# The last feed-forward block's gate and up projections as seven half-size products in place of eight

## The chip, the cores and the metric

The kernel runs on one core of a Trainium2 chip. The metric is the device time of one execution in microseconds; the median of three runs is compared. In the profile the engines are called PE (TensorE, matrix products), PEld (its weight loads), DVE (VectorE), ACT (ScalarE), POOL (GpSimd) and SP (SyncE, which issues the DMAs).

## What is computed

Two layers run over 512 latent and 256 context tokens of width 1024. Each layer has a feed-forward block, a token-mixing block and a second feed-forward block:

```python
def swiglu(h, wg, wu, wd):
    return (jax.nn.silu(h @ wg) * (h @ wu)) @ wd

def half_ffn(h, g, shift, scale, gate, wg, wu, wd):
    return h + 0.5 * gate * swiglu(modulate(rms_norm(h, g), shift, scale), wg, wu, wd)
...
        x = x + ml[5] * y_l
        x = half_ffn(x, g_norm[l, 2], ml[6], ml[7], ml[8], ffn_w_gate[l, 1], ffn_w_up[l, 1], ffn_w_down[l, 1])
        if need_ctx:
            ctx = ctx + mc[5] * y_c
            ctx = half_ffn(ctx, g_norm[l, 2], mc[6], mc[7], mc[8], ffn_w_gate[l, 1], ffn_w_up[l, 1], ffn_w_down[l, 1])
```

The hidden width is 2816, that is 22 tiles of 128. In the last layer `need_ctx` is false, so the fourth and last feed-forward block works on the 512 latent tokens alone; the other three work on all 768.

## The kernel before, in words

Activations lie transposed, as blocks of 128 channels by tokens. Every float32 operand of a projection is split into a high part (a rounded copy, made by ACT) and a low part (the rest, made by DVE), and each product is three matmuls: high weight by high data, high by low, low by high (`mm3`, L285). A weight tile arrives from memory as float32, 128 by 1024; `wsplit` (L200) casts it on ACT (`wh`) and subtracts on DVE (`wl`). So every weight tile costs both engines time, whatever the number of tokens.

`ffn` (L553) has two forms.

**Classical** (`classical`, L563). A hidden tile needs the projections of `h` by its gate weights and by its up weights: 2 projections of 8 channel blocks and 3 matmuls each, 48 matmuls, of 512 columns in the last block. Then silu of the gate on ACT, the product with up on DVE, and a split into high and low (`ah`, `al`). DVE and ACT split two weight tiles per hidden tile.

**Seven products** (L618 to L986; Winograd's variant of Strassen's form). The channels are halved (blocks 0 to 3 and 4 to 7), the tokens are halved, and gate and up are the two halves of the output. Of the eight block products seven are left, each of 4 channel blocks and 3 matmuls, 12 matmuls of half the tokens (`seventh`, L714): 84 matmuls of 384 columns for 768 tokens. For this, sums of halves of `h` are made and split once per block (`sums(j)`, L621, for four pairs of channel blocks; `sums_late`, L642, then overwrites a half of `h`), and sums of the weights for every hidden tile: `Weights` (L670) loads gate (`wr`, two buffers) and up (`wu`, one buffer) and makes four operands: `w1` the gate, `w2` two sums of up and gate (`ws`), `w3` what is left of up, `w4` half a tile of gate. These are four splits in place of two (three of 1024 columns and one of 512) and four DVE additions of 512 columns.

`Tile` (L725) holds a hidden tile. Its products p1, p6, p7 and p4 add into one PSUM bank B one after the other; between them ACT copies what has been added so far out of B (`take1` after p1, `take2` after p6, `take3` after p7), so the next one of them may begin only when that copy has ended. p2 goes to A; p5 and p3 go to C. `gate1`, `up2`, `act1`, `gate2` and `act2` put the pieces together on DVE, `high` and `low` split the result.

The order of PE, DVE and ACT in this form is written by hand: `chain` (L75) binds each instruction to the one before it on its engine. Hidden tiles go in groups of three (the last of four), `FAST`, L27. I call the tiles of a group a, b, c. PE's order in a group: p6, p2, p7, p5, p4 of a; p1, p2, p6, p5, p7 of b, p3 of a, p4 of b; the same for c, with p3 of b; p3 of c. While tile j runs, DVE and ACT make the weights of tile j+1 (`nx`), and finish tile j-1 (`p`). The gate weights of a tile are loaded when a buffer of `wr` is free, which is after the `w4` split two tiles before; its up weights are loaded when the split of the tile before's `w3` has ended.

After each group follows the **down** stage (L960): 8 output blocks, 3 matmuls per hidden tile each, with the update of the residual `xT` on DVE after each block. p1 of the next group's first tile is done in it.

In the kernel before, the last block does not take this form: `if not fast` (L602) runs the classical one in three groups of 8, 7 and 7 hidden tiles (`CHUNKS`, L25), each followed by its down stage through `residual` (L411). There the order on the engines is left to the scheduler.

The modulation vectors are worked off a queue beside the feed-forward blocks (`pump`, and `mod_step` in the seven-product form, two DVE steps `mr` and `mscr` each). In the trace the queue is empty when the last block's second hidden tile begins.

Of the kernel before, what the change touches and what calls it, by code (L numbers as in the profile page):

```python
# [24 lines left out]
CHUNKS = ((0, 8), (8, 7), (15, 7))  # L25
# [22 lines left out]
def tile_net(ctx: ExitStack, tc: tile.TileContext, a, out):  # L48
# [504 lines left out]
    def ffn(l, f, hin, streams, nxt, pre, npump, late={}):  # L553
# [5 lines left out]
        fast = w == T  # L559
        view = tv if fast else nv  # L560
        res = None

        def classical(m, ahead):  # L563
# [13 lines left out]
            else:  # L577
                pts = [ps(), ps()]
                for j in range(2):
                    project(full(pts[j]) if fast else plain(pts[j], cols), wgu[j], h)  # L580
                parts = [(banks(pts[0]), banks(pts[1]), pairs) if fast else
# [39 lines left out]
        def sums(j):  # L621

            X, Y = temp(), temp()
            lo, hi = slice(0, HALF), slice(HALF, T)
            c = slice(HALF * (j % 2), HALF * (j % 2) + HALF)
# [4 lines left out]
            ve.tensor_add(X, f32(h[j][0]), f32(h[j][1]))  # L630
            ve.tensor_add(Y, f32(h[j + 4][0]), f32(h[j + 4][1]))
# [7 lines left out]
            se.copy(U[j][0], Y)  # L639
            ve.tensor_sub(U[j][1], Y, f32(U[j][0]))  # L640

        def sums_late():  # L642

            hi = slice(HALF, T)
            for j in range(4):
                T1 = t1[j // 2][:, HALF * (j % 2):HALF * (j % 2) + HALF]
                se.copy(h[j][0][:, hi], T1)
                ve.tensor_sub(h[j][1][:, hi], T1, f32(h[j][0])[:, hi])

        chunks = FIRST if i == 0 else FAST  # L650
        sums_at = (2, 3, 4, 5) if i == 0 else (0, 1, 2)
        for ci in range(nslow):
# [14 lines left out]
            residual(down(m0, n), acts, gate, streams, None, view=tv)  # L667
# [41 lines left out]
        b11 = [tuple(t[:, 0:HALF] for t in h[k]) for k in range(4)]  # L709
        s1 = [tuple(t[:, HALF:T] for t in h[k]) for k in range(4)]  # L710
        b21 = [tuple(t[:, 0:HALF] for t in h[k + 4]) for k in range(4)]
        b22 = [tuple(t[:, HALF:T] for t in h[k + 4]) for k in range(4)]
# [1213 lines left out]
```

## Time and profile before

| | us |
|---|---|
| median of 3 runs | 2803.58 |
| range of these runs | 2801.41 to 2809.58 |
| the profiled execution's own time | 2802.09 |
| its span in the trace | 2800.0 |
| third feed-forward block, a group of three tiles with its down stage | 68.6 |
| last block, from its second hidden tile to PE's last matmul (2443.5 to 2795.3 in the trace) | 351.8 |

Times in the trace count from the start of the span. Nearly every instruction is recorded at line 66, a helper, so one goes by the names of tiles: `wl<-wr,wh` is the low part of a gate weight tile, `wl<-ws,wh` and `wl<-wu,wh` those of `w2` and `w3`, `w<-wr,w` that of `w4`; `s<-t` is `high` or `low` of a hidden tile; `t<-po` and `t<-ps` read PSUM. A timeline row gives start, duration, engine, operation and, in brackets, how long the engine stood idle before it and what ended that. DVE and ACT instructions overlap a little: the next one starts some 0.08 us before the one ahead of it ends.

### The profile page before, as it was taken

To read this page: it belongs to the slowest core of one execution; us is meant where nothing else is said; L and a number is where in the kernel's file an instruction comes from. 1 tells how busy PE (TensorE), PEld (TensorE's weight loads), DVE (VectorE), ACT (ScalarE), POOL (GpSimd) and SP (SyncE) were. 2 spreads that over 40 slices of the span, in tenths; PEclk is the share of its full clock that TensorE was granted. 3 is DMA by queue.
4 is the path that set the end of the run, shared out by engine and by line. 5 is a ranking of instruction groups with operands and counts; after the bars stand their busy time and mean duration, and the time that the engine had idled before them with its cause. 6 is when DMAs were issued, how large, how long until landed. Compare 5 with 4: busy or idle time off the path is not lost.

```text
span 2800.0 us, 38772 instructions
## 1 busy us (share of the span) xinstructions
PE 2705.3 (97%) x15364; PEld 2514.1 (90%) x15364; DVE 1949.8 (70%) x3279; ACT 1088.0 (39%) x1857; POOL 182.5 (7%) x224
## 2 busy tenths in 40 slices
PE   8999999999988999999999999999999999999999
PEld 5999999978878879999999899999988888888887
DVE  6756777777787877777778777776766788633333
ACT  5223333332477623333334333333332577322221
POOL 0000000010232200000000000000011132000000
PEclk9999999999999999999999999999999999999999
DMA  6322333215000332233333133333224102332232
GB/s 237 110 68 92 99 99 98 87 66 161 32 1 9 101 103 67 88 103 98 99 104 108 48 92 103 98 106 102 85 72 157 32 8 79 115 99 92 91 98 90
DMA packets 95268, 251.79 MB, mean 90 GB/s; under 512 B 11376, under 2 KB 40816, under 8 KB 95088
## 3 DMA queue, kind: packets, MB, share of 16 engines
q1 hardware_dynamic: 95088, 249.33, 28.1%
q8 instruction: 121, 1.98, 0.3%
q14 instruction: 59, 0.48, 0.1%
HBM read 247.19 MB, written 2.10 MB: 89 GB/s over the span
## 4 chain that ended last, share of the span: by engine, by line
PE 78%; DVE 10%; ACT 5%; DMA 3%; issue 2%; POOL 0%; SPq 0%; DVEq 0%; ACTq 0%; POOLq 0%
PE ps L66 46%; PE po L66 32%; DVE s L66 4%; ACT t L66 3%; DMA mr<-in_wm_dram 2%; DVE m L66 1%; ACT s L66 1%; DVE mr L66 1%; DVE t L66 1%; DMA wr<-in_wiN_dram 1%; DVE mscr L66 1%; DVE wl L66 1%; DVE xT L66 1%; ACT ph L66 1%; ACT ot L66 0%
## 5 line engine op out<-in xcount | busy, mean ns | idle before, releaser
L66 PE MATMUL ps<-s,wh 128*128 128x384 f32 (+2 forms) x4756 | 1153.0, 349 | 4.0 <-DVE t L66 2.1
L66 PEld LDWEIGHTS ps<-s,wh 128*128 128x128 f32 x4756 | 842.8, 189 | 73.1 <-DVE t L66 2.5
L66 PE MATMUL ps<-s,wl 128*128 128x384 f32 (+2 forms) x2378 | 714.3, 348 | 2.9 <-DVE wl L66 2.9
L66 PE MATMUL po<-s,wh 128*128 128x384 f32 (+2 forms) x2524 | 660.1, 343 | 2.4 <-ACT t L66 1.7
L66 PEld LDWEIGHTS po<-s,wh 128*128 128x128 f32 x2524 | 457.5, 188 | 18.3 <-ACT t L66 2.7
L66 PEld LDWEIGHTS ps<-s,wl 128*128 128x128 f32 x2378 | 433.6, 189 | 35.9 <-DVE wl L66 3.6
L66 PE MATMUL po<-s,wl 128*128 128x384 f32 (+2 forms) x1262 | 433.0, 343 | 7.2 <-DVE wl L66 7.2
L66 ACT CAST wh<-wr 128x1024 fp32r<-128x1024 f32 (+4 forms) x222 | 212.5, 959 | 413.8 <-PE ps L66 289.8
L66 DVE TENSOR_TENSOR wl<-wr,wh 128x1024 fp32r<-128x1024 f32 (+5 forms) x217 | 241.6, 1115 | 173.2 <-ACT wh L66 170.8
L66 DVE SCALAR_TENSOR_TENSOR xT<-ps,mod,xT 128x256 f32<-128x256 f32 (+1 forms) x392 | 213.1, 584 | 192.3 <-PE ps L66 191.9
L66 PEld LDWEIGHTS po<-s,wl 128*128 128x128 f32 x1262 | 237.8, 188 | 15.8 <-DVE wl L66 8.4
L66 DVE SCALAR_TENSOR_TENSOR mr<-mr,sb 128x1024 f32<-128x1024 f32 x128 | 156.1, 1219 | 6.7 <-DMA mr<-in_wm_dram 6.4
L66 PE MATMUL po<-s,s 128*128 128x256 f32 (+3 forms) x880 | 141.9, 314 | 11.5 <-ACT s L66 5.0
L66 ACT ACTIVATE t<-t 128x384 f32<-128x384 f32 x106 | 55.7, 525 | 243.4 <-DVE t L66 243.4
L66 ACT COPY t<-po 128x384 f32<-128x384 f32 (+1 forms) x161 | 76.9, 478 | 185.4 <-PE po L66 184.3
L66 PEld LDWEIGHTS po<-s,s 128*128 128x128 f32 x880 | 128.1, 192 | 19.4 <-ACT s L66 7.2
L66 DVE TENSOR_TENSOR t<-ps,t 128x384 f32<-128x384 f32 (+3 forms) x91 | 55.3, 607 | 119.3 <-PE ps L66 119.3
L337 POOL TENSOR_TENSOR s<-s,t 128x256 f32<-128x256 f32 x19 | 17.5, 921 | 1750.2 <-ACT t L66 1749.8
L66 ACT CAST s<-t 128x768 fp32r<-128x768 f32 (+2 forms) x129 | 88.0, 684 | 100.2 <-DVE t L66 100.0
L66 DVE TENSOR_TENSOR s<-t,s 128x768 fp32r<-128x768 f32 (+2 forms) x129 | 98.7, 767 | 37.9 <-ACT s L66 37.5
L66 DVE SCALAR_TENSOR_TENSOR mscr<-mr,sb 128x1024 f32<-128x1024 f32 x96 | 117.3, 1222 | 7.9 <-DMA mr<-in_wm_dram 6.3
L66 PE MATMUL po<-s,w 128*128 128x384 f32 x636 | 119.4, 336 | 0.0
(186 smaller groups left out, 3275.2 us busy)
## 6 DMA issues: line engine op xcount, KB each, us to landing
mr<-in_wm_dram SPq DMA_DIRECT2D x128, 512.0 KB, 3.7
wr<-in_wg_dram SPq DMA_DIRECT2D x88, 512.0 KB, 3.5
wu<-in_wu_dram SPq DMA_DIRECT2D x53, 512.0 KB, 3.5
t<-in_wd_dram SPq DMA_DIRECT2D x56, 384.0 KB, 3.5
wr<-in_wu_dram SPq DMA_DIRECT2D x35, 512.0 KB, 3.5
wr<-in_wiT_dram SPq DMA_DIRECT2D x22, 512.0 KB, 3.9
wr<-in_wd_dram SPq DMA_DIRECT2D x16, 512.0 KB, 3.5
wr<-in_wo_dram SPq DMA_DIRECT2D x14, 512.0 KB, 4.3
```

What stands on the lines that cost most here:

```text
L66: f(*args, **kw)
L337: (eng or ve).tensor_add(self.acc[:, :self.w], self.acc[:, :self.w], sq[:, :self.w])
```

## The change

The last block runs the seven-product form too, over halves of 256 tokens in place of 384. The classical branch for it goes, and `FAST` sets its groups: a first group of three classical tiles, during which `sums` run, then 19 tiles in five groups of three and one of four, so seven down stages in place of three. `nslow` and `sums_at` are those of the second and third block. The names `w` and `fast` become `w` (the number of tokens, 512 here), `hw` (its half) and `joint` (both streams).

```diff
-CHUNKS = ((0, 8), (8, 7), (15, 7))
...
-        fast = w == T
-        view = tv if fast else nv
-        res = None
+        joint = w == T
+        view = tv if joint else nv
+        hw = w // 2
+
+        def whole(pt):
+            return full(pt) if joint else plain(pt, cols)
...
-        if not fast:
-            for ci, (m0, n) in enumerate(CHUNKS):
-                acts = []
-                for m in range(m0, m0 + n):
-                    acts.append(classical(m, {}))
-                    if m < 18:
-                        pump(npump)
-                if ci == 0:
-                    pump(upto=gate)
-                lastc = ci == len(CHUNKS) - 1
-                if lastc:
-                    before_last()
-                res = residual(down(m0, n), acts, gate, streams, nxt if lastc else None, pre, late if lastc else {})
-            return res
...
-            lo, hi = slice(0, HALF), slice(HALF, T)
-            c = slice(HALF * (j % 2), HALF * (j % 2) + HALF)
+            lo, hi = slice(0, hw), slice(hw, w)
+            c = slice(hw * (j % 2), hw * (j % 2) + hw)
...
-                te.matmul(out=out[:, 0:HALF], lhsT=st[:, c], rhs=m, start=new and k == 0 and p == 0,
+                te.matmul(out=out[:, 0:hw], lhsT=st[:, c], rhs=m, start=new and k == 0 and p == 0,
...
         def update(o, pt):
+            if not joint:
+                x = tv(xT[o], LAT)
+                ve.scalar_tensor_tensor(out=x, in0=cv(pt, LAT), scalar=mod[gate][0][:, o:o + 1], in1=x, op0=ALU.mult, op1=ALU.add)
+                return
             v = banks(pt)
...
-                        project(full(pts[j]), D[0].w[j], acts, range(n - 1))
+                        project(whole(pts[j]), D[0].w[j], acts, range(n - 1))
```

Up to the last block's second hidden tile the engines' orders are the same as before. From there PE has 1596 matmuls of 256 columns (19 tiles of 84) in place of 912 of 512 (19 of 48); the 528 of the down stages stay.

On DVE, in the middle of the block, a hidden tile is two weight splits, one product and one low part before (`t` by `ps` is the product with up):

```order
L66 TENSOR_TENSOR s_23841<-t_23837,s_23840 128x512
L66 TENSOR_TENSOR wl_23922<-wr_23919,wh_23921 128x1024
L66 TENSOR_TENSOR t_23906<-ps_23857,t_23906 128x512
L66 TENSOR_TENSOR wl_23985<-wr_23982,wh_23984 128x1024
L66 TENSOR_TENSOR s_23910<-t_23906,s_23909 128x512
```

After the change, from `gate1` of a group's second tile b to the `w3` split of its third tile c, these rows stand on DVE (`wr_23880` and `wu_23896` are c's gate and up weights, `t_23667` is tile a, `t_23861` tile b):

```order
L65 TENSOR_TENSOR t_23861<-ps_23882,t_23861 128x256
L65 TENSOR_TENSOR wl_23927<-wr_23880,wh_23926 128x1024
L65 TENSOR_TENSOR ws_23942<-wu_23896 128x512
L65 TENSOR_TENSOR ws_23942<-ws_23942,wr_23880 128x512
L65 TENSOR_TENSOR wu_23896<-wr_23880,wu_23896 128x512
L65 TENSOR_TENSOR t_23958<-po_23912,t_23958 128x256
L65 TENSOR_TENSOR wl_23962<-ws_23942,wh_23961 128x1024
L65 TENSOR_TENSOR t_23667<-po_23821,t_23667 128x256
L65 TENSOR_TENSOR w_23979<-wr_23785,w_23979 128x512
L65 TENSOR_TENSOR t_23667<-t_23834,t_23667 128x256
L65 TENSOR_TENSOR wr_23880<-wr_23880,ws_23942 128x512
L65 TENSOR_TENSOR t_23861<-po_23862,t_23861 128x256
```

The `w3` split `wl_24000<-wu_23896` is the row behind the last. With the low part of a result, 14 DVE instructions now make the round of one tile where four made it: five on 256 columns, one on the result, the rest on weights.

On ACT a hidden tile is two weight casts, a silu and a cast of the result before:

```order
L66 CAST wh_23852<-wr_23850 128x1024
L66 ACTIVATE t_23837<-ps_23787 128x512
L66 CAST wh_23915<-wr_23913 128x1024
L66 CAST s_23840<-t_23837 128x512
L66 CAST wh_23921<-wr_23919 128x1024
```

After the change the same stretch as above reads on ACT, up to `take1` of tile c (`t_23984<-po_23985`):

```order
L65 CAST wh_23926<-wr_23880 128x1024
L65 COPY t_23958<-po_23862 128x256
L65 CAST wh_23961<-ws_23942 128x1024
L65 ACTIVATE t_23667<-t_23667 128x256
L65 CAST w_23979<-wr_23785 128x512
L65 CAST wh_23999<-wu_23896 128x1024
L65 CAST s_24003<-t_23667 128x512
L65 COPY t_23984<-po_23985 128x256
```

The copy that frees bank B for p6 of tile c stands behind the cast of tile a's result, and so behind everything that DVE does before `act2` of tile a.

More of the change, by code (lines that the diff above doesn't have):

```diff
@@ L638, in sums @@
             U[j] = slot(F32R), slot(F32R)
[L639 to L640 removed]
+            se.copy(U[j][0][:, :w], Y)
+            ve.tensor_sub(U[j][1][:, :w], Y, f32(U[j][0])[:, :w])
         def sums_late():
[L644 removed]
+            hi = slice(hw, w)
             for j in range(4):
[L646 removed]
+                T1 = t1[j // 2][:, hw * (j % 2):hw * (j % 2) + hw]
                 se.copy(h[j][0][:, hi], T1)
@@ L666, in ffn @@
                 pump(upto=gate)
-            residual(down(m0, n), acts, gate, streams, None, view=tv)
+            residual(down(m0, n), acts, gate, streams, None, view=view)
         W = {}
@@ L707, in split_fourth @@
                 self.w4 = t[:, 0:512], t[:, 512:1024]
[L709 to L712, printed above, removed]
+        b11 = [tuple(t[:, 0:hw] for t in h[k]) for k in range(4)]
+        s1 = [tuple(t[:, hw:w] for t in h[k]) for k in range(4)]
+        b21 = [tuple(t[:, 0:hw] for t in h[k + 4]) for k in range(4)]
+        b22 = [tuple(t[:, hw:w] for t in h[k + 4]) for k in range(4)]
         def seventh(out, wb, at, mv, new, end=True):
@@ L817, in ffn @@
         t2 = [tuple(t[:, hi] for t in U[j]) for j in range(4)]
-        t3 = [tuple(t[:, HALF * (j % 2):HALF * (j % 2) + HALF] for t in V[j // 2]) for j in range(4)]
-        w.split_gate()
-        w.sums()
-        w.split_sums()
-        w.fourth()
+        t3 = [tuple(t[:, hw * (j % 2):hw * (j % 2) + hw] for t in V[j // 2]) for j in range(4)]
+        wt.split_gate()
+        wt.sums()
+        wt.split_sums()
+        wt.fourth()
         chain("te", "ve", "se")
@@ L958, in weights @@
                     return D[q].w[o % 2]
-                return residual(weights, acts, gate, streams, nxt, pre, late, tv, ntail=6)
+                return residual(weights, acts, gate, streams, nxt, pre, late, view, ntail=6)
             for q in range(4):
```

23 lines of the change are left out of this document (12 added, 11 removed).

## The prediction

> **What bounds the kernel now.** I read the page first, for the share of each engine:
>
> ```profile
> PE 2705.3 (97%) x15364; PEld 2514.1 (90%) x15364; DVE 1949.8 (70%) x3279; ACT 1088.0 (39%) x1857; POOL 182.5 (7%) x224
> PE 78%; DVE 10%; ACT 5%; DMA 3%; issue 2%; POOL 0%; SPq 0%; DVEq 0%; ACTq 0%; POOLq 0%
> ```
>
> PE is busy nearly throughout. The chain that ended last, in order of time (start, length, what), shows the stretch that the change touches:
>
> ```profile
> 2443.52 351.74 PE ps L66 x1528
> 2795.26 0.02 issue
> 2795.28 0.48 DVE xT L66
> ```
>
> The last block is one unbroken run of PE. Then the busy times by stretch (length; PE, PEld, DVE, ACT, POOL busy; granted clock), for a three-tile group of the third block, which has the new form already, and for the last block:
>
> ```profile
> 1722.10:1790.70 68.60, 68.60 (x397) 68.60 (x397) 52.89 (x84) 23.28 (x35) 0.00 (x0) 1.00 0.32 101
> 2443.50:2795.30 351.80, 351.74 (x1529) 283.95 (x1527) 121.39 (x153) 86.74 (x105) 0.00 (x0) 1.00 0.31 95
> ```
>
> In both PE never rests. But the third block's group has DVE busy for 52.89 of 68.60 us, the last block only for 121.39 of 351.80. The question is whether DVE and ACT can follow when the same weights meet 512 tokens instead of 768.
>
> **What PE saves.** PE's timeline gives the pitch of matmuls that follow each other without a gap, two and one per row:
>
> ```profile
> 2371.93 0.63 PE L66 MATMUL ps<-s,wh 128*128 128x512 f32 x2
> 2392.93 0.63 PE L66 MATMUL ps<-s,wh 128*128 128x512 f32 x2
> 2393.63 0.39 PE L66 MATMUL po<-s,wh 128*128 128x256 f32 x2
> 2401.45 0.39 PE L66 MATMUL po<-s,wh 128*128 128x256 f32 x2
> ```
>
> 30 triples in 21.00 us make 0.2333 us for 512 columns, 23 triples in 7.82 us make 0.1133 us for 256. Each matmul has its own weight load in either case, so the smaller one loses nothing to that. A tile costs 48 x 0.2333 = 11.20 us of PE before and 84 x 0.1133 = 9.52 after; 19 tiles save 31.9 us if PE stays the bound. The down stages keep their 528 matmuls; a group of three tiles has 72, 16.8 us. So a group with its down stage takes 3 x 11.20 + 16.8 = 50.4 us before, and PE alone would take 45.4 after.
>
> **What DVE and ACT need.** The third block's trace has the same order of instructions, so its rows show the round that a middle tile makes, from one `w3` split (`wl<-wu`) to the next:
>
> ```profile
> 1721.51 1.21 DVE L66 TENSOR_TENSOR wl<-wu,wh 128x1024 fp32r<-128x1024 f32 x1
> 1722.75 1.22 DVE L66 SCALAR_TENSOR_TENSOR mscr<-mr,sb 128x1024 f32<-128x1024 f32 x1
> 1723.90 0.55 DVE L66 TENSOR_TENSOR t<-ps,t 128x384 f32<-128x384 f32 x1
> 1726.36 1.23 DVE L66 TENSOR_TENSOR wl<-wr,wh 128x1024 fp32r<-128x1024 f32 x1 [0.77 <-ACT wh L66]
> 1732.93 0.69 DVE L66 TENSOR_TENSOR w<-wr,w 128x512 fp32r<-128x512 f32 x1 [1.10 <-ACT w L66]
> 1735.08 1.21 DVE L66 TENSOR_TENSOR wl<-wu,wh 128x1024 fp32r<-128x1024 f32 x1
> ```
>
> and ACT's side of it:
>
> ```profile
> 1724.49 0.52 ACT L66 ACTIVATE t<-t 128x384 f32<-128x384 f32 x1 [3.98 <-DVE t L66]
> 1724.92 0.46 ACT L66 COPY t<-po 128x384 f32<-128x384 f32 x1
> 1725.28 1.05 ACT L66 CAST wh<-wr 128x1024 fp32r<-128x1024 f32 x1
> 1734.13 0.84 ACT L66 CAST s<-t 128x768 fp32r<-128x768 f32 x1 [0.27 <-DVE t L66]
> 1734.87 0.48 ACT L66 COPY t<-po 128x384 f32<-128x384 f32 x1
> ```
>
> The round takes 1735.08 - 1721.51 = 13.57 us. PE needs 14.56 there (68.60 less a down stage of 144 at 68.60 / 396 = 0.1732, through three), so it hides. What becomes of it in the last block: the modulation steps are gone, but only the first counts (1.15 us), since the second lies in the wait for `gate1`, silu, `take2` and the cast of `wr`, which follow each other across the two engines. Prices for 256 and 512 columns:
>
> ```profile
> L66 DVE TENSOR_TENSOR t<-po,t 128x256 f32<-128x256 f32 x1 | 0.4, 425 | 1.0 <-PE po L66 1.0
> L66 ACT ACTIVATE t<-ps 128x256 f32<-128x256 f32 x1 | 0.4, 374 | 0.0
> L66 DVE TENSOR_TENSOR s<-t,s 128x512 fp32r<-128x512 f32 x21 | 14.4, 684 | 0.0
> L66 ACT CAST s<-t 128x512 fp32r<-128x512 f32 x21 | 13.0, 621 | 0.2
> ```
>
> Against the 384-column rows each of the five DVE pieces shrinks by 0.125 us, each silu by 0.14, the copy (estimated with the silu) by 0.08: about 1.0 us together. 13.57 - 1.15 - 1.0 = 11.4 us. To that comes the load of the gate weights. It is issued when a's `w4` split ends, and takes
>
> ```profile
> wr<-in_wg_dram SPq DMA_DIRECT2D x15, 512.0 KB, 3.6
> ```
>
> 3.6 us. Walked through with these durations (time 0 is p6 of tile a), that split ends at 10.2, the weights are there at 13.8, and ACT could have cast them at 13.2: 0.6 us more. So the round is 12.0 us (11.4 to 12.5), against 9.52 of PE. **In the middle of a group DVE and ACT, taking turns, are the bound, not PE**, and 12.0 is more than the 11.20 of the classical tile.
>
> The walk through a group, by the same rows: b's `wl<-wu` begins at 11.0 and ends at 12.25; `take1` of b stands on ACT behind the cast for it and lets p6 of b begin at 10.1 instead of 9.5; `take2` stands behind silu and `gate1`, p7 begins at 13.3 instead of 12.8. PE is through p2 of tile c at 20.1. p6 of c needs `take1` of c, behind the cast of a's `act2`, as in the last two ACT rows above: `act2` ends at 22.2, the cast at 22.9, the copy at 23.2. PE stands still for 3.1 us. Six products later, at 31.4, it begins the down stage, does what a and b give (12 x 0.2333, and 0.3 for b's low part) until 34.5, and waits for the last low part of c: DVE and ACT have 10.6 us of work after `gate1` of c at 25.3 (next gate's split, `w4`, the down weights' split, then b's and c's results in turn), so 35.9. From there 5 matmuls, p1 of the next group (1.36) and 54 more make 51.0 us. A group is **51.0 against 50.4: the saving is eaten up**, before the clock is counted.
>
> **The clock.** Three gaps of PE and the stretches behind them, timeline first, then length, PE busy and granted clock:
>
> ```profile
> 2406.25 0.88 PE L66 MATMUL po<-ones,s 128*128 128x2 f32 x4 [2.03 <-DVE s L66]
> 856.87 0.63 PE L66 MATMUL po<-ident,s 128*96 128x128 f32 x2 [3.10 <-DVE s L66]
> 2222.96 0.55 PE L66 MATMUL po<-ident,t 128*128 128x128 f32 x3 [1.09 <-ACT t L66]
> ```
>
> ```profile
> 2406.30:2412.90 6.60, 6.60 (x31) 0.51 0.23 79
> 856.90:859.70 2.80, 2.80 (x14) 0.50 0.00 0
> 2223.00:2226.00 3.00, 3.00 (x25) 1.00 0.01 3
> ```
>
> After 2.03 and 3.10 us of idling PE runs at half clock for 2.8 to 6.6 us; after 1.09 it doesn't. So the 3.1 us stall in each group should cost half speed behind it: 1.4 to 3.3 us of PE. Part of that falls into the wait for c's results; what is left lengthens a group by 0.5 to 1.75 us. I take 1.1, the middle: in length the coming gap is nearest to the second row, in the dense stream around it to the first.
>
> The Trainium skill (TensorE: Matmul & The Clock Gate, "HAM oscillation — how this bites in real kernels") asks for idle gaps of over about 3.4 us before the clock falls. By it a 3.1 us gap would cost nothing, and the sum below would be +6.7 us. The row with 2.03 us, behind which the clock was 0.51, speaks against it.
>
> **The way in and out.** The three classical tiles end as before, at 2459.3 by these DVE rows (product with up, low part):
>
> ```profile
> 2459.35 0.69 DVE L66 TENSOR_TENSOR t<-ps,t 128x512 f32<-128x512 f32 x1 [3.55 <-PE ps L66]
> 2461.32 0.69 DVE L66 TENSOR_TENSOR s<-t,s 128x512 fp32r<-128x512 f32 x1
> ```
>
> Now a down stage follows at once, in which 6 matmuls (1.4 us) stand ahead of the third tile's result, which takes 0.69 + 0.62 + 0.68 and hops, 2.1 us: 0.7 us idle. During that stage DVE has the rest of the `sums`, 16 updates and the first tile's weights, about 17 us, beside PE's 16.8: 0.8 more before p6 (bounds 0 and 3; nothing here can gain). So the first p6 begins at 2459.3 + 16.8 + 1.36 + 1.5 = 2479.0. The last group has one middle tile more (12.0) and ends without a next p1: p3 of its last tile at 43.5, 2.1 us of waiting for the result (9 matmuls stand ahead), 96 x 0.2333 = 22.4: 68.0. The 8 more DMAs on SP carry the same bytes in smaller pieces and are issued ahead of need, behind no wait of their own; if one were late, a down stage would wait up to the 3.6 us above. The 32 more updates on DVE lie in down stages, where DVE has room.
>
> **Sum**: 2479.0 + 5 x 51.0 + 68.0 = 2802.0 for PE's last matmul, against 2795.3: +6.7 us. The clock in six groups, 6 x 1.1 = 6.6. Together +13.3: the profiled execution's own 2802.09 becomes 2815.4, and as the median of the runs lies 1.5 above it, **2816 to 2817; I say 2816**.
>
> **Rivals.** (1) *The clock holds* through 3.1 us. For it: that idle is shorter than one of the two gaps with evidence, and work is dense around it, unlike there. +6.7 gives 2809 to 2810, which a measurement can't tell from no change (0.3% is 8.4 us). Chance 0.22. The Trainium skill's section named above would have it so.
> (2) *PE stays the bound*, the other side. It decides in the middle of a group: the round from `wl<-wu` to `wl<-wu` would have to fit into 9.5 us. For it: by sums alone DVE has room, 14 pieces a tile are 8.8 us (durations less the 0.08 by which they overlap: 3 x 1.15, 5 x 0.345, 6 x 0.6), and in the third block PE never waits. Against: the round above already has 1.9 us of waits for ACT, which don't shrink. The price: 31.9 saved less 1.5 on the way in, 2773. Chance 0.06.
> (3) *More stalls*: half clock for 6.6 us behind each gap (1.75 a group), a few hundredths more at each of some 20 hand-overs between DVE and ACT (0.7 a group): 6.7 + 6 x 2.45 = 21.4, 2825. Chance 0.20.
> (4) *It doesn't do what it says*: the order has 1596 matmuls of 256 columns more and 912 of 512 fewer, so next to nothing, 0.02.
> The forecast itself has 0.50.
>
> **The numbers.** Faster by over 0.3% is (2) and half of (4): 0.07. Within 0.3% is (1) and the other half: 0.23. Slower is forecast and (3): 0.70. The range goes from the clock that holds with a group 0.8 us shorter than walked (+2, 2805) to (3) with 1 us more on the way in (2827); it leaves out (2) and the edges of the others.
>
> **What would show it.** Right: PE no longer in one run; in each group one idle of about 3 us ahead of a 256-column `po<-s,wh`, ended by ACT's copy of `t` from `po`; granted clock well below 1 behind it; `wl<-wu` to `wl<-wu` 12 us apart in mid-group; groups of 51 to 53 us. Wrong: gaps that stay under 1.5 us, or groups near 46 us, then the round was overrated; a clock of 1.00 behind 3 us gaps, rival (1); weights that land late (`wr` or `wu` from DMA as the releaser), then the load is the bound.

## The result, and the profile after

| | before | after |
|---|---|---|
| median of four runs each | 2802.49 us | 2829.15 us |
| range | 2792.76 to 2809.58 | 2825.30 to 2835.76 |
| ratio of the times, 95% interval | | 1.009 (1.0062 to 1.0117) |

The change makes the kernel slower, by 27 us (17 to 33 by the interval), where 13 were forecast; 2829 us lies above the forecast's range of 2805 to 2827. The profiled execution of after took 2835.76 us. It comes to the last block 10.94 us later than the one of before (the 48 matmuls `ps<-s,we` ahead of it start at 2441.45 instead of 2430.51), in instructions that the change leaves alone. The traces of the sixteen runs below, with the same instructions up to there, reach this point between 2412.15 and 2442.54, so that lead is spread of the runs. From those matmuls to the last matmul it is 387.65 us against 364.8: **+22.9 us**, and this is the number to explain by the trace.

The last block, by stretches that begin with p6 of each group's first tile (length; PE, PEld, DVE, ACT, POOL busy; granted clock):

```profile
2489.76:2544.36 54.60, 49.36 (x324) 44.20 (x325) 37.70 (x56) 20.83 (x35) 0.00 (x0) 0.97 0.27 88
2544.36:2597.03 52.67, 47.30 (x325) 42.44 (x324) 37.01 (x55) 20.89 (x35) 0.00 (x0) 1.00 0.26 90
2597.03:2650.93 53.90, 49.29 (x326) 44.31 (x324) 37.18 (x55) 21.10 (x35) 0.00 (x0) 0.97 0.27 89
2650.93:2705.27 54.34, 48.83 (x325) 43.89 (x324) 37.26 (x55) 21.10 (x35) 0.00 (x0) 0.97 0.27 88
2705.27:2759.26 53.99, 49.11 (x325) 44.18 (x324) 37.16 (x55) 21.00 (x35) 0.00 (x0) 0.97 0.27 88
2759.26:2829.10 69.84, 63.21 (x421) 56.98 (x419) 43.64 (x70) 25.31 (x42) 0.00 (x0) 0.98 0.29 94
```

A group of three takes 53.9 us (mean of five), where 52.1 were forecast with the clock and 50.4 is the classical form. No engine is full: PE rests for 5 us, DVE for 17. What PE waits for from 2436 on (total, times, longest; the 1.1 us for `s` is the wait ahead of `ps<-s,we`, which the kernel before has too):

```profile
PE po L65 <- ACT t L65: 26.3, 20, 3.6
PE ps L65 <- ACT s L65: 5.0, 6, 1.1
PE ps L65 <- DVE xT L65: 2.9, 7, 1.2
```

and where that falls in the fourth group (PE's rows behind a wait, in order: p6 of b, p7 of b, p6 of c, c's result in the down stage):

```profile
2661.45 0.50 PE L65 MATMUL po<-s,wh 128*128 128x256 f32 x2 [0.83 <-ACT t L65]
2664.70 0.50 PE L65 MATMUL po<-s,wh 128*128 128x256 f32 x2 [0.15 <-ACT t L65]
2675.34 0.50 PE L65 MATMUL po<-s,wh 128*128 128x256 f32 x2 [3.56 <-ACT t L65]
2689.11 0.96 PE L65 MATMUL ps<-s,wh 128*128 128x512 f32 x2 [0.77 <-ACT s L65]
```

This is the picture that the prediction drew: one idle of over 3 us in each group, ahead of p6 of c, ended by ACT's copy. The rows of DVE around it, from one `wl<-wu` to the next:

```profile
2662.38 1.22 DVE L65 TENSOR_TENSOR wl<-wu,wh 128x1024 fp32r<-128x1024 f32 x1
2663.51 0.42 DVE L65 TENSOR_TENSOR t<-ps,t 128x256 f32<-128x256 f32 x1
2666.27 1.23 DVE L65 TENSOR_TENSOR wl<-wr,wh 128x1024 fp32r<-128x1024 f32 x1 [2.34 <-ACT wh L65]
2668.20 0.69 DVE L65 TENSOR_TENSOR ws<-wu 128x512 f32<-128x512 f32 x1 [0.70 <-DMA wu<-in_wu_dram]
...
2675.22 1.22 DVE L65 TENSOR_TENSOR wl<-wu,wh 128x1024 fp32r<-128x1024 f32 x1
```

The round is 12.84 us (12.60 to 12.84 over the six groups), not 12.0, and the row with 0.70 is one that the prediction did not have: DVE waits for the **load** of the next up weights. The chain of waits has that load in every group (two of its pieces):

```profile
2653.27 3.79 DMA wu<-in_wu_dram
2663.62 4.48 DMA wu<-in_wu_dram
```

It can be issued only when `wl<-wu` has read the buffer's last content, and lands up to 4.5 us later beside the load of the gate weights. In five of the six groups `ws` of c waits 0.40 to 0.70 us for it; in the second the gate load, which took 4.06 us there, ends the wait. Last, the stretches of some 5.5 us behind the six stalls (3.12, 3.53, 3.08, 3.56, 3.42 and 3.39 us):

```profile
2514.45:2520.00 5.55, 5.55 (x34) 5.55 (x35) 3.86 (x5) 2.14 (x4) 0.00 (x0) 0.69 0.65 248
2568.52:2574.00 5.48, 5.48 (x46) 5.48 (x47) 3.79 (x6) 3.06 (x6) 0.00 (x0) 1.00 0.67 246
2621.07:2627.00 5.93, 5.93 (x38) 5.93 (x39) 3.79 (x5) 2.25 (x4) 0.00 (x0) 0.71 0.62 233
2675.34:2681.00 5.66, 5.66 (x35) 5.66 (x36) 3.80 (x5) 2.25 (x4) 0.00 (x0) 0.70 0.66 248
2729.40:2735.00 5.60, 5.60 (x35) 5.60 (x36) 3.86 (x5) 2.14 (x4) 0.00 (x0) 0.70 0.66 244
2783.57:2789.00 5.43, 5.43 (x33) 5.43 (x34) 3.26 (x4) 1.62 (x3) 0.00 (x0) 0.69 0.54 186
```

Behind five of them the clock is about 0.7, behind the second, one of the longest, it stays at 1.00, and the number of matmuls in the stretch (46 instead of 34) says the same.

### The profile page after: what moved, and what is told of

It is laid out like the page before. It is cut to its first block, busy times and chain, and to the rows that moved or that the text cites. A ratio compares the mean times of both kernels' runs of the same rounds, so it can differ in the third digit from the quotient of the medians.

```text
span 2833.9 us, 40609 instructions
## 1 busy us (share of the span) xinstructions
PE 2703.9 (95%) x16048; PEld 2543.5 (90%) x16048; DVE 2094.0 (74%) x3543; ACT 1146.6 (40%) x1997; POOL 182.9 (6%) x224
## 3 DMA queue, kind: packets, MB, share of 16 engines
q1 hardware_dynamic: 99312, 249.33, 26.7%
## 4 chain that ended last, share of the span: by engine, by line
PE 71%; DVE 13%; ACT 7%; DMA 6%; issue 3%; POOL 0%; SPq 0%; ACTq 0%; DVEq 0%; POOLq 0%
PE ps L65 37%; PE po L65 34%; DVE s L65 3%; ACT t L65 3%; DMA mr<-in_wm_dram 2%; DVE wl L65 2%; DVE t L65 2%; ACT s L65 2%; DVE m L65 1%; ACT wh L65 1%; DMA wu<-in_wu_dram 1%; DVE mr L65 1%; DMA s<-in_wm_dram 1%; DVE ws L65 1%; DVE xT L65 1%
## 5 line engine op out<-in xcount | busy, mean ns | idle before, releaser
L65 PE MATMUL ps<-s,wh 128*128 128x384 f32 (+2 forms) x4300 | 993.1, 340 | 10.6 <-ACT s L65 4.3
L65 PE MATMUL po<-s,wh 128*128 128x384 f32 (+2 forms) x3284 | 808.1, 332 | 28.7 <-ACT t L65 28.0
L65 PEld LDWEIGHTS po<-s,wh 128*128 128x128 f32 x3284 | 581.9, 190 | 49.6 <-ACT t L65 32.9
L65 PE MATMUL po<-s,wl 128*128 128x384 f32 (+2 forms) x1642 | 544.6, 332 | 7.9 <-DVE wl L65 7.9
L65 DVE SCALAR_TENSOR_TENSOR xT<-ps,mod,xT 128x512 f32<-128x512 f32 (+1 forms) x416 | 235.7, 604 | 143.1 <-PE ps L65 142.4
L65 DVE TENSOR_TENSOR wl<-wr,wh 128x1024 fp32r<-128x1024 f32 (+3 forms) x186 | 200.4, 1080 | 126.6 <-ACT wh L65 126.6
L65 PE MATMUL po<-s,s 128*128 128x256 f32 (+3 forms) x880 | 141.5, 313 | 11.9 <-ACT s L65 5.1
L65 PE MATMUL po<-s,w 128*128 128x384 f32 (+1 forms) x864 | 150.1, 322 | 0.0
L65 DVE TENSOR_TENSOR t<-po,t 128x384 f32<-128x384 f32 (+2 forms) x226 | 117.9, 522 | 31.4 <-ACT t L65 30.7
L65 PEld LDWEIGHTS po<-s,w 128*128 128x128 f32 x864 | 140.5, 188 | 0.0
L65 DVE TENSOR_TENSOR s<-t,s 128x768 fp32r<-128x768 f32 (+3 forms) x143 | 104.2, 730 | 48.6 <-ACT s L65 48.1
```

Source lines behind the costliest of these rows:

```text
L65: f(*args, **kw)
```

## The experiments

Theory at the start: DVE's and ACT's turns bound a group, as predicted, and the load of `wu` and the clock make the rest. Rivals: the cut into groups costs, not the product form; or the loss is only the place of one copy in ACT's order. All lengths of a group below run from a wait of PE to the same wait in the next group; in the change they are 52.6, 54.0, 54.3 and 54.1 us.

**1. The groups alone.** The kernel before with seven groups:

```diff
-CHUNKS = ((0, 8), (8, 7), (15, 7))
+CHUNKS = ((0, 3), (3, 3), (6, 3), (9, 3), (12, 3), (15, 3), (18, 4))
```

> The classical kernel before the change, with its last feed-forward cut into seven groups of 3, 3, 3, 3, 3, 3 and 4 tiles instead of three of 8, 7 and 7: seven down stages, no products of half size. My theory (the product form's chain between VectorE and ScalarE makes the loss, the groups next to none): per added down stage at most the wait for the last tile's result, which is covered by 6 matmuls of 0.2333 us (1.4 us) against its 2.1 us, so 0.7 us, four times: +3 us, between 0 and +5. Rival (the cut into groups makes a large part of the loss, through the extra down stages, updates and down weights in small pieces): +10 us or more, and TensorE waits for `wd` or for the updates.

Measured: ratio 1.0015 (0.9999 to 1.0030) to before; in the trace the block takes 367.9 us against 364.8, +3.1. PE's waits in it:

```profile
PE ps L66 <- DVE xT L66: 0.8, 2, 0.4
```

So the groups cost about 3 us, as expected; the rest of it lies in gaps too short for this list. The other 20 or so of the 22.9 belong to the product form.

**2. The copy earlier.** `take1` ahead of the cast of `wu` and of a's result, in the last block alone (the expectation names the cast of `ws`, but that one still stands ahead of the copy):

```diff
                 p.act1()
                 t.w.split_up()
...
+                if not joint:
+                    t.take1()
...
                 t.p2()
-                t.take1()
+                if joint:
+                    t.take1()
```

> The changed kernel, with one instruction moved in the last block's groups: ScalarE's copy of the next tile's first product (`take1`) ahead of the casts of `ws` and of the tile's result instead of behind them. My theory (VectorE's and ScalarE's round of 12 to 13 us as a whole bounds a group): the third tile's sixth product starts up to 1.5 us sooner, its gap shrinks from some 3.4 us to about 2, but the next wait, for the third tile's seventh product or its result, grows by nearly as much; a group keeps its 53 to 54 us within 1 us, the kernel 0 to -6 us against the change. Rival (the place of that copy in ScalarE's order is the cause): the stall of 3.4 us and the low clock behind it both go, 4 us a group and more, -25 us, so as fast as the kernel before or faster.

Measured: 1.0076 (1.0051 to 1.0102), groups of 52.8, 52.5, 52.9 and 52.6 us. PE's two waits in tile c, p6 and p7:

```profile
2613.42 0.50 PE L65 MATMUL po<-s,wh 128*128 128x256 f32 x2 [1.65 <-ACT t L65]
2617.92 0.50 PE L65 MATMUL po<-s,wh 128*128 128x256 f32 x2 [1.50 <-ACT t L65]
```

The stall of 3.4 us became one of 1.65 and one of 1.50. What the group gained, 1 us, is about what the low clock had cost. The rival that this copy alone is the cause falls.

**3. Two buffers for the up weights.** `mq` is free in the last block:

```diff
-                self.u = pool.tile([P, 1024], F32, name=nm("wu"), tag="mscr", bufs=1)
+                self.u = pool.tile([P, 1024], F32, name=nm("wu"), tag="mscr" if joint or self.m % 2 else "mq", bufs=1)
```

> The changed kernel, with the weights of up (`wu`) loaded into two buffers in turn instead of one, so that the load for a tile need not wait for the tile before. My theory (the load of `wu`, 4.3 to 4.5 us beside the load of `wr`, became part of the round, which the forecast had taken as off the path): VectorE's sum `ws` no longer waits for it (0.7 us in one group), the third tile's result comes 0.7 to 1 us sooner, a group shrinks by 0.7 to 1 us: about -6 us against the change, between -3 and -9. Rival (VectorE and ScalarE taking turns are the bound by themselves, the load ends beside it): the wait moves to the next instruction, no change beyond 2 us.

Measured: 1.0079 (1.0055 to 1.0103), which the times can't tell from the change's 1.0090. The trace can: from p6 of a to p6 of c it is 23.4 to 23.5 us in three of four groups, where the change has 24.0 to 24.4 and the walk had 23.2. The round shows it best (DVE, third group):

```profile
2606.61 1.21 DVE L65 TENSOR_TENSOR wl<-wu,wh 128x1024 fp32r<-128x1024 f32 x1
...
2618.69 1.21 DVE L65 TENSOR_TENSOR wl<-wu,wh 128x1024 fp32r<-128x1024 f32 x1
```

It is 12.08 us, and 12.04 to 12.09 in five of six groups, where nothing waits for `wu` any more; in the other the gate load took 4.72 us and the round 13.21. Groups of 54.3, 53.4, 51.9 and 52.0 us; the first two have a clock of 0.70 behind the stall (one of 3.63 us, one of 2.80), the others 1.00 (2.82 and 2.80 us). The two with 2.80 us:

```profile
2618.81:2624.50 5.69, 5.69 (x35) 5.69 (x36) 3.85 (x5) 2.14 (x4) 0.00 (x0) 0.70 0.65 238
2724.08:2730.00 5.92, 5.92 (x50) 5.92 (x51) 4.23 (x7) 3.25 (x6) 0.00 (x0) 1.00 0.63 231
```

So the load is on the round with about 0.7 us a group.

**4. The gap filled.** 20 matmuls whose results nothing uses, in a group's third tile (and in the fourth of the last group; the second tile, which the expectation names too, has none):

```diff
                 t.p2()
...
+                if not joint and j > 1:
+                    for _ in range(20):
+                        te.matmul(out=t.A[:, 512:512 + hw], lhsT=t.w.w1[0][:, 512:640], rhs=b21[0][0], start=True, stop=True)
```

> The changed kernel, with 20 extra matmuls of 256 columns in the gap ahead of the sixth product of every second or later tile of a group in the last block; their results are used by nothing, the rest is as before. They take 20 x 0.1133 = 2.3 us of a gap of 3.4 us and so leave about 1.1 us of it, which in the trace before did not lower the clock. At the second tile of a group, where the gap is only 0.3 to 0.8 us, they delay TensorE by up to 2 us, which the later wait takes up. Theory of the clock (the granted clock of 0.70 behind the gap costs 1 us a group or more): the clock stays at 1.00 behind it, and groups are 1 to 1.5 us shorter in spite of the useless work, -5 to -8 us against the change. Rival (the time that the low clock takes lies within the later wait for the third tile's result): groups stay within 0.5 us or get up to 1 us longer.

Measured: 1.0044 (1.0026 to 1.0061): faster than the change by some 0.45% with 140 useless matmuls in it (the two intervals meet at 1.006; in the trace the block takes 377.9 us against 387.65). Groups of 51.4, 52.3, 52.5 and 51.5 us. The wait ahead of p6 of c, and the clock behind it:

```profile
2671.13 0.51 PE L65 MATMUL po<-s,wh 128*128 128x256 f32 x2 [1.14 <-ACT t L65]
```

```profile
2671.13:2677.00 5.87, 5.87 (x50) 5.87 (x51) 4.18 (x7) 3.25 (x6) 0.00 (x0) 1.00 0.63 232
```

From p6 of c to c's result it is 12.33 us here. In the change it is 13.75 to 13.80 in the four groups with a low clock and 12.34 in the one without: the low clock costs 1.43 us each time, inside of the forecast's bounds (0.5 to 1.75).

**5 to 8. Splits earlier.** If the turns bound a group, the split of the up weights has to come sooner, too:

```diff
                 t.p4()
+                if not end and not joint:
+                    nx.split_up()
                 p.gate2()
...
                 p.act1()
-                t.w.split_up()
+                if joint:
+                    t.w.split_up()
+                else:
+                    t.take1()
```

> The changed kernel, with two instruction pairs moved in the last block's groups: the split of the next tile's up weights (ScalarE's cast and VectorE's `wl<-wu`) directly behind the split of `ws`, ahead of the silu of the second half, of `w4` and of the tile's result; and the copy `take1` ahead of the cast of the result, as in the run with that copy alone. My theory (what bounds a group is the order in which VectorE and ScalarE take turns between the arrival of `wu` and the seventh product, so a gap goes only if the copy and the split both come sooner): in the trace of the change `wl<-ws` ends at 2671.93 in the fourth group; `wl<-wu` could end at 2673.1 and the copy at 2672.2, so the third tile's sixth product starts at 2672.3 instead of 2675.34 and its seventh waits for nothing; the gap is under 1 us, the clock stays near 1.00 behind it, and a group takes 51 to 52.5 us instead of 54: -8 to -15 us against the change. Rival (VectorE's and ScalarE's work as a sum is the bound, whatever its order): the gap only moves, as with the copy alone, and the kernel stays within 4 us of the change.

The next three add the two buffers of run 3 (`e6_both`); then `nc.gpsimd` in place of `ve` in `fourth` (`e7_fourth_on_gpsimd`); or, without that, `nx.split_gate()` of a group's last tile behind `t.low(hi)` (`e8_gate_split_later`).

> The earlier split of the up weights and the earlier copy, and the up weights in two buffers in turn. My theory: once the order no longer delays it, the seventh product depends on the arrival of `wu`, and two buffers take that load off: 0.5 to 1 us a group less than with the new order alone, -3 to -6 us against that. Rival (the load is hidden as soon as the split comes earlier, since its buffer comes free earlier too): within 2 us of it.

> As the run with both, with the fourth weight sum (`wr<-wr,ws`, 0.68 us on VectorE) on GpSimd, which does nothing else in the last block. My theory (VectorE waits for ScalarE and loads in every round, so its sum is not the bound): within 2 us of the run with both; 0.6 us sooner on VectorE, given back at the hand-over to GpSimd and back. Rival (VectorE's sum is the bound now): 0.6 us less in each of 18 tiles, -8 to -11 us against the run with both.

> As the run with both, with the split of the next group's first gate weights (ScalarE's cast and `wl<-wr`, which waits for its load) moved from ahead of the last tile's result to behind it. My theory (the end of a group is bound by the work of VectorE and ScalarE ahead of the last tile's result, in which that split with its wait for the load is 1.1 to 2.3 us): the result comes 1 to 2 us sooner, TensorE's wait for it goes from 0.8 us or more to near 0, and the first product of the next group waits at most 0.7 us for the late split: 0.5 to 1.5 us a group, -2 to -7 us against the run with both. Rival (the first product waits for as much as the result gains): within 2 us.

Measured: 1.0146 (1.0116 to 1.0177), 1.0167 (1.0142 to 1.0192), 1.0167 (1.0139 to 1.0195) and 1.0149 (1.0124 to 1.0173); groups of 58 to 59, 57 to 58, 59 to 60 and 58 us. All are slower than the change (the block takes 409 to 418 us in the traces, against 387.65), which neither the theory nor its rival had. The trace of run 6 shows one reason, on SP, ACT and DVE:

```profile
2674.11 0.33 SPq L196 DMA_DIRECT2D wr<-in_wg_dram  x1
```

```profile
2678.53 1.05 ACT L65 CAST wh<-wr 128x1024 fp32r<-128x1024 f32 x1 [2.46 <-DMA wr<-in_wg_dram]
```

```profile
2679.61 1.22 DVE L65 TENSOR_TENSOR wl<-wr,wh 128x1024 fp32r<-128x1024 f32 x1 [4.25 <-ACT wh L65]
```

The gate load waits for the buffer that `w4` of an earlier tile is split from. With the up split ahead of it `w4` comes later, so does the load, and DVE stands still for 4.25 us. An order that helps one chain starved another. GpSimd's and the gate split's runs show no gain on top that can be measured (GpSimd takes 1.5 us for the sum that DVE does in 0.68), which speaks against DVE's sum and the end of the group as the bound there.

**9 to 11. Loads made free.** The fourth sum goes into `ws`, `w4` into `mq`, and the raw weights of gate and up go round three buffers:

```diff
+            def raw(self, k):
+                tag, bufs = (("wr", NWR), ("wr", NWR), ("mscr", 1))[(2 * self.m + k) % 3]
+                return pool.tile([P, 1024], F32, name=nm("wu" if k else "wr"), tag=tag, bufs=bufs)
...
-                ve.tensor_sub(self.g[:, 512:1024], self.g[:, 512:1024], self.s[:, 512:1024])
+                self.f = self.g if joint else self.s
+                ve.tensor_sub(self.f[:, 512:1024], self.g[:, 512:1024], self.s[:, 512:1024])
...
-                t = pool.tile([P, 1024], F32R, name=nm("w4"), tag="mr", bufs=2)
+                t = pool.tile([P, 1024], F32R, name=nm("w4"), tag="mr" if joint else "mq", bufs=2 if joint else 1)
```

For a group's first tile the fourth sum is written over half of `ws` ahead of its split, so `w2` of that tile holds other numbers, and runs 9 to 11 compute another result than the block; the instructions are as many and as long, so the times can be compared. Run 10 adds the new order of run 5, run 11 the later gate split to that.

> The changed kernel with the instructions of TensorE, VectorE and ScalarE in their old order, but other buffers in the last block: the fourth sum is written into the second half of `ws`, `w4` into a buffer of its own, and the raw weights of gate and up go round three buffers, so that a gate load waits for an up split of two tiles before and an up load for the fourth sum of the tile before, instead of each for the split one step ahead. The same number of bytes, loads and instructions. My theory, changed after the run with the new order (there the gate load was issued at 2674.11, when `w4` of the tile before had let go of its buffer, and the split of the gate weights waited 4.25 us for it): the two loads, each behind the split that frees its only free buffer, are a part of the round. Without them the wait of `wl<-wr` falls from 2.34 us to 1.4 or less and that of `ws` for `wu` goes; the third tile's sixth product comes 1.3 us sooner, a group takes 51 to 53 us: -6 to -15 us against the change. Rival (the turns of VectorE and ScalarE are the bound, the loads only fill their waits): groups stay at 53 to 54 us, within 4 us of the change.

> The free loads, and on top the new order that alone cost time: the split of the next tile's up weights and the copy `take1` sooner. My theory (the new order was slower only because it put off `w4` and so the gate load): with the loads free the third tile's sixth product starts at about the end of its second (no gap over 1 us), its seventh waits for nothing, and what is left of a group is TensorE's 45.4 us, the last result's wait of 2 to 3 us and some short ones: 48 to 50.5 us instead of 54, -20 to -32 us against the change, so between 8 us faster and 6 us slower than the kernel before. Rival (the new order is bad in itself, since it delays silu and the result): 56 us a group or more, as with the new order alone.

> As the last one, with the split of the next group's first gate weights behind the last tile's result instead of ahead of it. My theory (with the mid-group stalls gone, the end of a group is the largest wait left): TensorE's wait for the result shrinks by 0.5 to 1.5 us a group, -2 to -6 us against the last one. Rival (the first product of the next group then waits for that split, or the result is late for other reasons): within 2 us.

Measured: 1.0095 (1.0070 to 1.0120), 1.0153 (1.0131 to 1.0176) and 1.0165 (1.0141 to 1.0189); groups of 54.7, 56 to 57 and 56 to 58 us. The round of run 9 and a new wait (first two rows DVE, then ACT):

```profile
2663.42 1.22 DVE L65 TENSOR_TENSOR wl<-wu,wh 128x1024 fp32r<-128x1024 f32 x1
...
2674.83 1.22 DVE L65 TENSOR_TENSOR wl<-wu,wh 128x1024 fp32r<-128x1024 f32 x1
```

```profile
2682.40 0.62 ACT L65 CAST w<-ws 128x512 fp32r<-128x512 f32 x1 [3.69 <-PE po L65]
```

Without the loads the round is 11.41 us, 11.40 or 11.41 in all five groups of three: the walk's 11.4, so its hand-overs were right and the loads are the rest of the 12.84. But `w4`, now in one buffer, waits for PE in a group's last tile, and the end of the group loses what the middle won. The theory that freeing the loads is enough falls as well, and the late gate load is not the whole reason for runs 5 to 8: in run 10 no cast waits for it any more, and the order of run 5 still takes 56 to 57 us.

**12. A written order.** Runs 2 and 5 to 11 move one wait and get another. What is left to test is that the order as a whole is at fault. The five groups of three tiles get a table that names every instruction, and a loop that issues them (`H` a cast, `L` the low part, r, s, u and 4 the weights, then the tile):

```diff
+TABLE = ("p6.0 Hu.0 g.1 Lu.0 u.1 p2.0 Hr.1 take2.0 p7.0 Lr.1 p5.0 gate1.0 take3.0 s1.1 p4.0 s2.1 H4.0 "
...
+            if not joint and not lastc:
+                nt = tabled(m0, n, nt)
+                continue
```

> The changed kernel with the same instructions, buffers and loads, and TensorE's and the loads' order unchanged; only the order of VectorE's and ScalarE's instructions in the five groups of three tiles of the last block is written out anew, over a whole group. It was looked for by walking through the group with the durations of the trace of the change (loads 3.8 to 4.6 us, 0.07 to 0.16 us for a hand-over), moving one instruction at a time as long as TensorE's waits got shorter: splits of the next weights come as early as their load allows, the copies `take1` and `take2` at once behind their product, the parts of a tile's result later. The walk gives 53 to 58 us a group for the order of the change and 46.0 to 48.6 for the new one. My theory, changed again (neither the sum of VectorE's and ScalarE's work nor a single load bounds a group, but the order, in which each engine waits for the other while it has other work that could go first): groups of 46 to 49 us, 5 x 5 to 8 us less than the change, -25 to -38 us, so 0 to 12 us faster than the kernel before. Rival (the sum is the bound, so that any order gives another wait, as the moved split did): groups of 52 us or more, no faster than the change by more than 8 us.

Measured: 1.0056 (1.0033 to 1.0079); groups of 53.0, 53.9, 52.1 and 51.3 us. The middle of the group has one wait of 1.3 us left, but the result of c comes late, since ACT stands ahead of it for a load of down weights:

```profile
2620.47 0.83 ACT L74 CAST wh<-t 128x768 fp32r<-128x768 f32 x1 [3.85 <-DMA t<-in_wd_dram]
```

**13, 14. Two more orders, and the loads in the written order.** Other tables, and the sync engine's DMAs chained like the other engines' instructions (`chain("sy")` around the loop).

> As the run with the written order, with another order for VectorE and ScalarE, and with the loads issued in the written order too. The walk, now with buffers that are taken as they come free, gives 53.1 to 55.7 us a group for the order of the change (measured 52.6 to 54.3), 50.1 to 51.6 for the first written order (measured 51.3 to 53.9, two thirds of it with a low clock behind a stall) and 46.5 to 48.3 for this one, with no stall of TensorE over 1.2 us that could lower the clock. My theory (the order is the cause): groups of 46.5 to 49 us, -25 to -37 us against the change, so 0 to 12 us faster than the kernel before. Rival (VectorE's and ScalarE's work as such): groups of 51 us or more, as with the first written order, no more than 10 us less than the change.

> The same with a second order from the same walk, in which the splits of the down weights come later and those of the next tile's weights sooner; the walk gives 46.4 to 48.4 us a group. My theory: within 1 us a group of the other order, -25 to -37 us against the change. Rival: one of the two has stalls of over 2 us that the walk doesn't know, and is slower by 2 us a group or more; then the walk lacks a wait, and the size of the order's part stays open.

Measured: 0.9962 (0.9942 to 0.9982) and 0.9962 (0.9946 to 0.9977), 10.7 us **faster** than the kernel before (in the trace of run 13 the block takes 353.9 us against 364.8). Groups of run 13, from p6 of b to p6 of b, with the same columns as above:

```profile
2484.43:2530.90 46.47, 45.85 (x324) 42.27 (x325) 36.39 (x55) 21.01 (x36) 0.00 (x0) 1.00 0.31 103
2530.90:2577.39 46.49, 45.88 (x324) 42.29 (x324) 36.76 (x56) 21.10 (x36) 0.00 (x0) 1.00 0.30 102
2577.39:2624.25 46.86, 46.24 (x325) 42.74 (x325) 36.81 (x56) 21.00 (x36) 0.00 (x0) 1.00 0.32 102
2624.25:2670.96 46.71, 46.21 (x325) 42.46 (x325) 37.02 (x56) 20.99 (x36) 0.00 (x0) 1.00 0.31 102
```

DVE and ACT are as busy as in the change, 36.8 and 21.0 us, in 46.6 us instead of 53.9; PE rests for 0.6 us in a group. What is different is to be seen on ACT, from the cast of `ws` of tile c on. The change (cast of `ws`, silu of a's second half, `w4`, cast of `wu`, a's result, `take1`):

```profile
2669.70 1.05 ACT L65 CAST wh<-ws 128x1024 fp32r<-128x1024 f32 x1 [2.95 <-DVE ws L65]
2672.38 0.42 ACT L65 ACTIVATE t<-t 128x256 f32<-128x256 f32 x1 [1.63 <-DVE t L65]
2672.70 0.60 ACT L65 CAST w<-wr 128x512 fp32r<-128x512 f32 x1
2673.21 1.04 ACT L65 CAST wh<-wu 128x1024 fp32r<-128x1024 f32 x1
2674.40 0.62 ACT L65 CAST s<-t 128x512 fp32r<-128x512 f32 x1
2674.92 0.36 ACT L65 COPY t<-po 128x256 f32<-128x256 f32 x1
```

and run 13 (`ws`, `w4`, `take1`, a's result, `wu`):

```profile
2589.43 1.05 ACT L74 CAST wh<-ws 128x1024 fp32r<-128x1024 f32 x1 [0.96 <-DVE ws L74]
2590.38 0.61 ACT L74 CAST w<-wr 128x512 fp32r<-128x512 f32 x1
2590.91 0.36 ACT L74 COPY t<-po 128x256 f32<-128x256 f32 x1
2591.17 0.62 ACT L74 CAST s<-t 128x512 fp32r<-128x512 f32 x1
2591.69 1.05 ACT L74 CAST wh<-wu 128x1024 fp32r<-128x1024 f32 x1
```

From the cast to the end of the copy it is 5.58 us there and 1.84 here: the silu, which waits 1.63 us for DVE, no longer stands between, since the second half of a had its silu ahead of the cast of `ws`.

**15, 16. One of the two alone.** Run 15 is the change with only the loads in the written order, run 16 is run 13 with the loads left to the scheduler.

> The changed kernel with VectorE and ScalarE in its own order, and only the loads of the five groups issued in the order in which the code is written (the second and third load of the down weights ahead of the next group's second gate load, and so on) instead of the order in which the scheduler put them. My theory (the order of VectorE and ScalarE is the cause): groups stay at 52.5 to 54.5 us, within 4 us of the change. Rival (a load that was issued late was the cause): groups of 50 us or less, -15 us or more.

> The faster of the written orders for VectorE and ScalarE (the first of the two that keep the loads in order), with the loads again as the scheduler puts them. My theory: most of the gain stays, groups of 46.5 to 50 us, but a down load that the scheduler puts behind a gate load that waits may cost 2 to 3 us a group, as with the first written order. Rival (the loads' order is the cause): groups of 52 us or more.

Measured: 1.0098 (1.0071 to 1.0125) with groups of 54.9, 54.0, 52.5 and 53.9 us; 0.9950 (0.9927 to 0.9973) with groups of 47.2, 46.5, 46.5 and 46.9 us. The order of DVE and ACT is the cause; that of the loads alone does nothing. (The intervals of runs 13 and 16 overlap, so which of these two is better stays open.) The group of four tiles has the old order in these runs too, in runs 13, 14 and 16 with a stall of 3.5 to 3.6 us and a clock of about 0.7 behind it, so this is not the last word.

## Why the prediction was right or wrong

- **"In the middle of a group DVE and ACT, taking turns, are the bound, not PE"**: right for this order. PE rests in each group ahead of p6 of c, ended by ACT's copy, as written. Run 9 has the round without loads at the 11.4 us that the prediction added up, run 3 the round with the gate load alone at its 12.0 (12.04 to 12.09).
- **The way in**: right. p6 of the first group starts at 2489.76, less 10.94 is 2478.8, forecast 2479.0. Seven down stages instead of three cost little, which run 1 shows by itself (+3.1 us).
- **The round of 12.0 us, and so p6 of c at 23.2: this is the step that failed.** It put the load of the gate weights on the round (0.6 us) and gave the load of `wu` no term at all, without a reason; what it calls "issued ahead of need" is eight more loads of down weights. The load of `wu` has one buffer, is issued behind `wl<-wu`, and takes 4.25 to 4.48 us beside the gate load in the six groups. With the 3.6 us that the prediction took for the gate load it would have landed at 2667.22 in the fourth group, in time for `ws` at 2667.50 (an estimate from its issue at 2663.62); at 4.48 us it is late. The round was 12.60 to 12.84 us; without the wait for `wu` (run 3) it is the forecast's. The round also begins late: b's `wl<-wu` starts 11.3 to 11.9 us behind p6 of a, forecast 11.0, and why stays open. Together p6 of c starts 24.0 to 24.7 us behind p6 of a, 1.1 more on the mean, times five. Run 3 gets 0.7 of it back. The prediction named weights that land late as a sign that it was wrong, but gave them no price.
- **From p6 of c on**: 12.34 us to c's result without the clock, and about 0.6 us on to its low part (that wait is in the 0.96 us of the row at 2689.11): 12.9 against 12.7. From there to the next group 15.6 against 15.1; 0.2 of that is a wait for `xT` that the walk did not have; the other 0.3 is not traced.
- **The clock**: 1.1 a group forecast; 1.43 in four groups of five and 0 in one are 1.14. Rival (1), the clock holds, is out as a rule; it came true once in six stalls.
- **Rival (3), more stalls**, came nearest in size (21.4 us for the 22.9 in the trace), but with other terms: 1.75 a group for the clock and 0.7 for hand-overs, where the traces have 1.14 for the clock and 1.8 for the rest, over half of it ahead of p6 of c.
- **The sum**: -0.2 for the way in, 5 x 1.8 for the groups (53.9 for 52.1), +0.7 for the last group (69.84 for 69.1) are +9.5 on the 13.3: 22.8 of the 22.9 us in the trace. The medians differ by 26.7; the last 4 are within the interval of the ratio.
- **Rival (2), PE stays the bound**, was judged by its condition (a round within 9.5 us) against the waits "which don't shrink". They shrink: in runs 13, 14 and 16 a group takes 46.3 to 47.2 us, 45.4 of it PE's own. The prediction walked through one order, found 1.9 us of waits in it, and took them for a property of the work. As a forecast of this change it was right to give that rival little; as a judgment of what the form can do it was not.

## What to carry to other kernels

Here two engines took turns, neither was full, and the order in which each took its instructions was the bound, not their sum. Moving one or two instructions only moved the wait (seven runs); writing the order of a whole period anew removed it. So an order that was made for a larger tile (here 768 tokens, where PE hides the turns) is worth making again for a smaller one. In a walk every load that has one buffer belongs on the round, from the instruction that frees the buffer to the landing, with its time beside other loads.

## What the runs showed of the hardware

- The granted clock behind a stall of PE is not a matter of its length alone. In the change stalls of 3.08 to 3.56 us were followed by 0.69 to 0.71, one of 3.53 by 1.00. In run 3 one of 2.80 us was followed by 0.70, another of 2.80 by 1.00. In run 9 stalls of 2.12 to 2.14 us were followed by 0.69. In run 2 stalls of 1.65 and 1.50 us, 3 us apart, left it at 1.00. But 1.09 us, behind which the prediction's row has 1.00, is no safe length either: in the same trace PE waits 1.11 us ahead of `ps<-s,we` at 2430.51, and the clock is 0.50 over the next 5.5 us. The Trainium skill (TensorE: Matmul & The Clock Gate, "HAM oscillation — how this bites in real kernels") asks for idle gaps of over about 3.4 us before the clock falls; the rows disagree on both sides, and on what it does depend stays open here.
- In the change the load of c's up weights (512 KB), issued 2.1 us behind a gate load, took 4.25 to 4.48 us in the six groups; that of b's, by itself, took 3.54 to 3.85 us.
- Matmuls that do nothing, put into a stall, can make a kernel faster: 20 of them in each group took 0.45% off (run 4); the clock behind the stall stayed at 1.00.
